# Modulation weights requested one step ahead in a two-layer hybrid decoder

## The chip, the cores and the metric

The kernel runs on one core of a Trainium2 chip. Its time is the device time of one execution in microseconds (us). Engines: PE is TensorE (matrix products), PEld its weight loads, DVE is VectorE, ACT is ScalarE, POOL is GpSimd. SP is the sync engine, whose queue issues most DMAs here. Less time is better.

## The reference

Two layers work on x of 1024 tokens by 1024 channels, in float32. Each layer computes

```
mod = silu(c) @ W_mod + b_mod             # W_mod is 1024 x 3072: shift, scale, gate
h = rms_norm(x, pre_gain) * (1 + scale) + shift
proj = h @ W_in                           # 1024 x 3088 columns, for three groups of heads
a = sliding-window attention, r = retention, g = gated linear attention, each times silu of a gate
x = x + gate * rms_norm(concat(a, r, g) @ W_out, post_gain)
```

The modulation is the same for all tokens: one row of 1024 numbers times a matrix of 12 MB per layer. Shift and scale of a layer are wanted before its first projection, the gate only after its output projection.

## The kernel before

Every product of the trunk is split into a high and a low part, so each weight block and each input are held twice, and a projection is three runs of eight products. Weights come in blocks of 256 columns. `load` (L467) brings a block in four pieces of 256 KB through a ring of five staging buffers (tag `st`, `stage`, `BST` = 5); ACT or DVE makes the high part, DVE or POOL the low part (L491, L481), and that frees the staging buffer. The converted block lies in a place of `arenas` until PE reads it.

The modulation that is not needed at the very start is computed beside the other stages by `mod_third(l, j)` (L344), for layer l and third j (0 shift, 1 scale, 2 gate). It works in two passes of 512 columns. A pass has eight steps k. A step brings a slice of `W_mod`, 128 rows by 512 columns, 256 KB, into a buffer of the same staging ring (SP queue, the kind `lwm`), and DVE multiplies it by one column of silu(c) and adds it to `acc` (L365 for the first step of shift and scale, L367 otherwise). After the eighth step PE sums `acc` over the partitions by products with ones (the closing products). `acc` exists once, so a pass begins its multiplies only when PE has read the pass before. Eight passes run this way: the gate of layer 0, scale and shift of layer 1 during layer 0, and the gate of layer 1 during layer 1.

The order of PE's instructions is written out by the program: generators ("jobs") emit their instructions when a planner's clock (`clk`) has advanced far enough. The clock grows by a cost for each product, `pump` looks for jobs that are due, and `accum` calls it after every 7 products of 256 columns or every 4 of 512. After each part of its work a job says with `yield lat(name, l)` how many planned us must pass before the next; the numbers stand in the table `L` (`@1` marks layer 1). In `mod_third`, `mod7` is the distance from the request of a slice to its multiply, `mod2` the distance from a multiply to the next request, and `mod3` that from the last multiply to the closing products. The flag `modh` of the shift lets the jobs that normalise and transpose tokens for layer 1 (`pre`, transposes at L176) go on; the flag `mod` of the gate lets the output projection begin.

Only PE is ordered by hand (`tc.manual_schedule(engines={PE})`). The instructions of SP, DVE, ACT and POOL are ordered by the framework when the program is built, by readiness and free buffers, with the written order as rank. Each engine then carries out its own list strictly in that order, and an issue on SP that waits for a staging buffer holds back what stands behind it.

Other names that the text uses: `attn_turn` is the softmax of the attention (DVE L934 copies scores, L936 takes the maximum, ACT L939 the exponentials). `aoS` is attention output kept in HBM, read back by SP and used by DVE at L1445. L1209 is the masking of retention scores on DVE.

Of the kernel before, what the change touches and what calls it, by code (L numbers as in the profile page):

```python
# [23 lines left out]
KT = D // P  # L24
# [65 lines left out]
def trunk(ctx: ExitStack, tc: tile.TileContext, ins, cst, out):  # L90
# [14 lines left out]
    def nm(s):  # L105
        uid[0] += 1
        return f"{s}_{uid[0]}"

    def t2(dt=F32):
        return gp.tile([P, 512], dt, tag="t2", name=nm("t2"), bufs=B2)  # L110
# [4 lines left out]
    def stage():  # L115
        return gp.tile([P, 512], F32, tag="st", name=nm("st"), bufs=BST)
# [7 lines left out]
    def aux(dt=F32):  # L124
        return ps.tile([P, 512], dt, tag="aux", name=nm("aux"), bufs=8 - MMB)
# [23 lines left out]
    def dma(k, dst, src):  # L149
        {"S": nc.sync, "A": A, "P": G}[EN[k]].dma_start(dst, src)  # L150
# [9 lines left out]
    def mult(dst, lhsT, rhs, start, stop, cost=None):  # L160
        T.matmul(dst, lhsT, rhs, start=start, stop=stop)  # L161
        if cost is not None:
            clk[0] += cost
            return
        n = 1
        for d in rhs.shape[1:]:
            n *= d
        c = n / 2400.0
        if rhs.dtype == F32R:
            c = max(c, 0.107 if lhsT.shape[-1] > 64 else 0.055)  # L170
        else:
            c = max(4 * c, 0.21 if n > 2 else 0.03)
        clk[0] += c
# [5 lines left out]
    def lat(key, l):  # L179

        return L[key + "@1"] if l and key + "@1" in L else L[key]

# [3 lines left out]
    def flag(name, lat=0.0):  # L186
        flags[name] = clk[0] + lat
# [75 lines left out]
    def mod_rows(l, j, eng=nc.sync):  # L263
        rows = gp.tile([16, P], F32, tag="row", name=nm("rows"), bufs=2)
        eng.dma_start(rows[0:8, :], b_mod[l:l + 1, j * D:(j + 1) * D].rearrange("o (k p) -> (o k) p", p=P))
        eng.dma_start(rows[8:16, :], pre_g[l:l + 1, :].rearrange("o (k p) -> (o k) p", p=P))
        return rows

    def mod_rows_t(rows, pool=aux):
        pr = pool()  # L270
        transp(pr[:, 0:16], rows, ident[0:16, 0:16])
        rc = small(16)
        V.tensor_copy(rc, pr[:, 0:16])
        return rc

    def mod_cols(l, j, hh, pm, rc):
        res = modc[(l, j)]
        ks = slice(4 * hh, 4 * hh + 4)
        if j == 0:
            V.tensor_tensor(res[:, ks], pm[:, 0:4], rc[:, ks], ALU.add)  # L280
        else:
            col = small(4)
            V.tensor_tensor(col, pm[:, 0:4], rc[:, ks], ALU.add)
            V.scalar_tensor_tensor(res[:, ks], col, 1.0, rc[:, 8 + 4 * hh:12 + 4 * hh], ALU.add, ALU.mult)

    def mod_tile(l, j):
        modc[(l, j)] = cp.tile([P, KT], F32, name=nm(f"mod{j}"), tag=f"mod{j}")
# [56 lines left out]
    def mod_third(l, j):  # L344
        wv = w_mod[l].rearrange("(p k) n -> p k n", k=KT)
        if j < 2:
            mod_tile(l, j)
            rows = mod_rows(l, j)
            yield lat("mod1", l)
            rc = mod_rows_t(rows)  # L350
        else:
            res = cp.tile([P, D], F32, name=nm("modg"), tag="modg")
            modg[l] = res
        for hh in range(2):
            c0 = j * D + 512 * hh
            acc = gp.tile([P, 512], F32, tag="acc", name=nm("acc"), bufs=1)
            if j == 2:
                G.memset(acc, 0.0)
                nc.sync.dma_start(acc[0:1, :], b_mod[l:l + 1, c0:c0 + 512])
            for k in range(KT):  # L360
                wt = stage()
                dma("lwm", wt, wv[:, k, c0:c0 + 512])
                yield lat("mod7", l)
                if k == 0 and j < 2:
                    V.tensor_scalar(acc, wt, c_act[:, k:k + 1], None, ALU.mult)  # L365
                else:
                    V.scalar_tensor_tensor(acc, wt, c_act[:, k:k + 1], acc, ALU.mult, ALU.add)  # L367
                yield lat("mod2", l)
            yield lat("mod3", l)
            pm = aux()  # L370
            if j < 2:
                for b in range(4):
                    mult(pm[:, b:b + 1], acc[:, b * P:(b + 1) * P], ones[:, 0:1], True, True)
                mod_cols(l, j, hh, pm, rc)
                if j == 0:
                    flag(("modh", l, hh), lat("mod4", l))
            else:
                mult(pm, ones, acc, True, True)
                gain = stage()
                nc.sync.dma_start(gain, post_g[l:l + 1, 512 * hh:512 * hh + 512].to_broadcast((P, 512)))  # L380
                V.tensor_tensor(res[:, 512 * hh:512 * hh + 512], pm, gain, ALU.mult)
            yield lat("mod5", l)
        flag(("mod", l, j), lat("mod6", l))

    def mod_all(l, js, after=None):
        if after is not None:
            yield (0.0, after)
        for j in js:
            yield from mod_third(l, j)
# [57 lines left out]
    def tables_T():  # L447

        for p in range(NP_):
            yield L["tt1"]  # L450
            rep_ = t2()
            V.tensor_copy(rep_.rearrange("p (s t h k) -> p s t h k", s=2, t=2, h=4),
                          sincos[:, 2 * p:2 * p + 2, :, 0:32].rearrange("p t s k -> p s t k").unsqueeze(3)
                          .to_broadcast((P, 2, 2, 4, 32)))
            yield L["tt2"]
            pt = aux()
# [127 lines left out]
    def pre(l, t, xt, early=False, soon=False):  # L584
# [9 lines left out]
        with ExitStack() as es:  # L594
# [3 lines left out]
            for j in range(2):  # L598
                if EN[f"xn{j}"] == "A" or early and XA[t][j] == "A" or soon and XA[t][j] == "A":
                    A.activation(xn[j], xt[j], AF.Copy, scale=r)  # L600
                else:
                    scaled[t] = V.tensor_scalar(xn[j], xt[j], r, None, ALU.mult)  # L602
        yield 0.5 if early else L["pf1"] if soon else lat("pre1", l)
        if early:
# [79 lines left out]
    def load_x(t, xt, eng_):  # L684
        for j in range(2):
            eng_.dma_start(xt[j], x_in[0, t * P:(t + 1) * P, 512 * j:512 * j + 512])

    def pre_first(t):
        xt = [t2(), t2()]
        load_x(t, xt, nc.sync)  # L690
        yield L["pf3"] + L["pf2"] * (t - 4)
        yield from pre(0, t, xt)
# [606 lines left out]
    def table_job():  # L1299
        more = True  # L1300
        yield (L["tb0"], ("hT", 0, TT))
        while more:
# [205 lines left out]
B2, B1, BS, BST, MMB, SMB = 12, 8, 11, 5, 3, 6  # L1508
EN = {"qst": "S", "smh": "S", "sml": "S", "sm0": "S", "sm1": "S", "lao": "S", "sao": "S", "lmix": "S", "ssg": "S", "lsg": "S", "ssr": "S", "lsr": "A", "lx": "S", "sx": "A", "lw": "S", "lwm": "S", "whi0": "V", "whi1": "A", "whi2": "A", "whi3": "A", "wlo0": "V", "wlo1": "G", "wlo2": "V", "wlo3": "G", "xn0": "V", "xn1": "V", "hlo0": "G", "hlo1": "V", "rot0": "V", "rot1": "V", "rdec": "V", "kslo": "V", "qslo": "V", "vlo": "G", "kT": "A", "qT": "A", "sprev": "A", "pn": "G", "pf0": "A", "aoc": "A", "hng": "V", "mh": "A", "gso": "V", "mg": "V", "mgl": "V", "rT": "A", "rv": "A", "gv": "A", "gk": "A", "ak0": "V", "ak1": "V", "ak2": "V", "ak3": "V", "kd0": "G", "kd1": "G", "kd2": "G", "kx1": "G", "kx2": "G", "kx3": "V", "kx4": "V", "qb": "G", "stx": "V"}
TURN = ("AV", "AV")  # L1510
L = {"tt1": 5.71, "tt2": 6.96, "tb1": 28.02, "tb2": 0.05, "pf3": 12.62, "pf1": 6.69, "pf2": 4.0, "mod1": 4.3, "mod2": 2.4, "mod3": 17.69, "mod4": 5.8, "mod5": 0.09, "mod6": 0.05, "pre1": 7.43, "kv1": 8.84, "kv2": 2.31, "aq1": 7.17, "aq7": 7.95, "ag1": 5.62, "aq2": 2.4, "aq6": 6.2, "aq3": 11.35, "aq4": 7.54, "aq5": 4.01, "hn1": 8.14, "hn2": 3.76, "gz1": 10.47, "gz2": 13.49, "gl1": 4.43, "gd3": 16.57, "gc1": 1.21, "gc2": 1.95, "gc3": 0.65, "gc4": 3.27, "gc6": 3.2, "gc5": 4.23, "rc1": 0.73, "rc2": 2.11, "rc3": 1.31, "rc4": 2.84, "fin1": 11.68, "lay1": 0.05, "mod2@1": 2.23, "mod3@1": 16.46, "mod5@1": 3.78, "mod6@1": 3.24, "pre1@1": 10.18, "kv1@1": 3.37, "kv2@1": 0.05, "aq1@1": 5.95, "aq7@1": 6.81, "ag1@1": 8.3, "aq2@1": 2.07, "aq6@1": 9.39, "aq3@1": 11.0, "aq4@1": 6.32, "aq5@1": 1.76, "hn1@1": 10.35, "hn2@1": 3.59, "gz1@1": 3.83, "gz2@1": 12.55, "gl1@1": 17.99, "gd3@1": 15.63, "gc1@1": 1.6, "gc2@1": 1.95, "gc3@1": 0.47, "gc4@1": 1.87, "gc6@1": 0.05, "gc5@1": 1.38, "rc1@1": 0.12, "rc2@1": 3.46, "rc3@1": 2.6, "rc4@1": 5.99, "fin1@1": 9.35, "lay1@1": 1.23, "gc7": 0.81, "gc7@1": 0.33, "tb0": 0.05, "mod7": 1.0, "mod7@1": 1.0}
CHUNK = 7
VDB = 8
VDF = 6
# [49 lines left out]
```

## Time and profile before

| | |
|---|---|
| median of 3 runs | 972.73 us (972.31 to 973.64) |
| profiled execution | 971.16 us, span 969.4 us, 1.8 us around it |
| PE busy | 951.3 us (98% of the span) |
| PEld busy | 829.4 us (86%) |
| DVE, ACT, POOL busy | 640.2, 410.1, 272.5 us |
| DMA | 140.30 MB, mean 145 GB/s |
| granted TensorE clock | 0.996 |

Times are counted from the start of the span. A row of a group gives line, engine, operation, written tile <- read tiles, shape and count, then busy us and mean ns of one, then the idle time of the engine just before these instructions and what ended it. A row of a wait list reads: who waited <- for whom: us in total, times, longest. A row of the timeline gives start, length, engine, line and operation, and in brackets the idle time before it. In the chain of waits a row gives start and length of the piece that the end depended on.

### The profile page before, as it was taken

Reading aid. Unit: us, or ns where it says so; the run is one execution under the profiler, and the core shown is the slowest. Engines: PE = TensorE matmul, PEld = TensorE weight load, DVE = VectorE, ACT = ScalarE, POOL = GpSimd, SP = SyncE. Lnnn points to the kernel's source line nnn. Section 1 sums busy time; section 2 is a strip of 40 time slices with the busy share of each in tenths; the row PEclk is TensorE's granted clock in tenths of the full one; section 3 lists DMA queues with packets and bytes.
Section 4 is the critical chain, followed back from the end, with each engine's and each line's share of the span. In section 5 each row is a group of like instructions: output and inputs, shape, how many; then the busy total and the mean of one; then the engine's idle time right before and its main releaser. Section 6 shows DMA issues by size and latency. Waiting matters only on the chain.

```text
span 969.4 us, 18061 instructions
## 1 busy us (share of the span) xinstructions
PE 951.3 (98%) x6513; PEld 829.4 (86%) x6513; DVE 640.2 (66%) x1525; ACT 410.1 (42%) x1119; POOL 272.5 (28%) x323
## 2 busy tenths in 40 slices
PE   6999999999999999999999999999999999999997
PEld 1799999989998877878889999998999887777886
DVE  6886857777777777655586485686776577763332
ACT  2777312354422666622455531134652166761111
POOL 3243011533430344511242110144423034441000
PEclk9999999999999999999999999999999999999999
DMA  9943314624335355677455160253222333555871
GB/s 313 320 146 110 111 56 129 187 77 112 115 102 150 98 168 180 218 242 237 172 166 172 50 180 22 83 155 92 80 86 77 120 88 105 158 174 174 261 238 65
DMA packets 124293, 140.30 MB, mean 145 GB/s; under 512 B 12734, under 2 KB 95528, under 8 KB 124204
## 3 DMA queue, kind: packets, MB, share of 16 engines
q1 hardware_dynamic: 116204, 127.43, 42.9%
q10 hardware_dynamic: 8000, 11.72, 3.4%
q8 instruction: 51, 0.84, 0.4%
q14 instruction: 38, 0.31, 0.1%
HBM read 102.42 MB, written 34.60 MB: 141 GB/s over the span
## 4 chain that ended last, share of the span: by engine, by line
PE 86%; DMA 7%; DVE 3%; issue 2%; POOL 1%; ACT 0%; SPq 0%; DVEq 0%; ACTq 0%; POOLq 0%
PE mm L161 67%; PE aux L161 15%; PE aux L176 4%; DMA wm<-in_w_mod_dram 2%; DMA t<-in_x_dram 1%; DMA st<-in_w_in_dram 1%; DMA xk<-in_x_dram 1%; DMA t<-aoS 1%; DMA st<-in_w_mod_dram 1%; POOL sm L529 1%; DVE acc L367 0%; DVE t L1292 0%; POOL arena L491 0%; DVE t L624 0%; DMA c_ident<-cst_ident_dram 0%
## 5 line engine op out<-in xcount | busy, mean ns | idle before, releaser
L161 PE MATMUL mm<-arena,arena 128*128 128x256 f32 (+2 forms) x1896 | 303.0, 315 | 1.4 <-ACT arena L628 0.7
L161 PE MATMUL mm<-arena 128*128 128x256 f32 (+2 forms) x1824 | 294.7, 317 | 0.0
L161 PEld LDWEIGHTS mm<-arena,arena 128*128 128x128 f32 x1896 | 261.8, 188 | 24.6 <-ACT arena L628 1.2
L161 PEld LDWEIGHTS mm<-arena 128*128 128x128 f32 x1824 | 255.4, 191 | 22.0 <-issue 1.2
L161 PE MATMUL mm<-arena,mx 128*128 128x512 f32 (+1 forms) x744 | 168.7, 386 | 0.0
L161 PEld LDWEIGHTS mm<-arena,mx 128*128 128x128 f32 x744 | 135.6, 188 | 29.1 <-issue 1.5
L529 POOL TENSOR_TENSOR sm<-sm,mhalf 128x4 f32<-128x4 f32 (+1 forms) x60 | 51.8, 863 | 294.8 <-DVE sm L528 285.3
L491 POOL TENSOR_TENSOR arena<-st,arena 128x512 fp32r<-128x512 f32 x55 | 80.3, 1467 | 91.3 <-ACT arena L145 34.7
L145 ACT ACTIVATE t<-aux 128x512 f32<-128x512 f32 (+1 forms) x96 | 48.7, 521 | 106.4 <-PE aux L176 44.9
L943 POOL TENSOR_TENSOR smx<-smx,sm 128x512 f32<-128x512 f32 x32 | 36.2, 1131 | 114.8 <-DVE sm L942 111.4
L491 DVE TENSOR_TENSOR arena<-st,arena 128x512 fp32r<-128x512 f32 x65 | 62.3, 969 | 4.7 <-PE mm L161 2.6
L145 ACT ACTIVATE arena<-st 128x512 fp32r<-128x512 f32 x82 | 48.5, 626 | 29.0 <-PE mm L161 13.0
L1247 ACT ACTIVATE t<-mm 128x512 f32<-128x512 f32 x30 | 17.9, 597 | 92.2 <-PE mm L161 40.3
L939 ACT ACTIVATE smx<-smx,sm 128x129 f32<-128x129 f32 x128 | 50.0, 393 | 14.0 <-DVE sm L936 13.9
L1248 DVE TENSOR_TENSOR t<-mm,modg 128x512 f32<-128x512 f32 x30 | 20.6, 689 | 48.6 <-ACT t L1247 48.5
L367 DVE SCALAR_TENSOR_TENSOR acc<-st,c_act,acc 128x512 f32<-128x512 f32 x60 | 47.3, 788 | 7.5 <-DMA st<-in_w_mod_dram 6.8
L1292 DVE SCALAR_TENSOR_TENSOR t<-t,sm,t 128x512 f32<-128x512 f32 x32 | 25.9, 846 | 39.7 <-DMA t<-xs 20.8
L176 PE MATMUL aux<-c_ident,t 128*128 128x128 f32 x288 | 45.5, 278 | 2.9 <-DVE t L602 2.9
L176 PEld LDWEIGHTS aux<-c_ident,t 128*128 128x128 f32 x288 | 34.9, 144 | 7.3 <-DVE t L602 4.2
L934 DVE COPY_PREDICATED smx<-c_curmask,aux 128x256 f32<-128x256 int32 x64 | 25.5, 447 | 15.0 <-ACT smx L145 10.4
L990 ACT ACTIVATE t<-aux 128x256 f32<-128x256 f32 x32 | 12.2, 382 | 54.1 <-PE aux L161 26.8
L995 DVE TENSOR_TENSOR t<-aux,sm 128x256 f32<-128x256 f32 x32 | 13.6, 425 | 30.8 <-POOL sm L529 30.8
(214 smaller groups left out, 1300.9 us busy)
## 6 DMA issues: line engine op xcount, KB each, us to landing
st<-in_w_in_dram SPq DMA_DIRECT2D x96, 256.0 KB
st<-in_w_mod_dram SPq DMA_DIRECT2D x64, 256.0 KB
mx<-mixS SPq DMA_DIRECT2D x30, 512.0 KB
mixS<-t SPq DMA_DIRECT2D x64, 128.0 KB
st<-in_w_out_dram SPq DMA_DIRECT2D x32, 256.0 KB
mixS<-t SPq DMA_DIRECT2D x32, 256.0 KB
wm<-in_w_mod_dram SPq DMA_DIRECT2D x12, 512.0 KB
t<-in_x_dram SPq DMA_DIRECT2D x24, 256.0 KB
```

Source lines behind the costliest of these rows:

```text
L145: A.activation(dst, src, AF.Copy)
L161: T.matmul(dst, lhsT, rhs, start=start, stop=stop)
L176: T.transpose(dst, src, idn)
L367: V.scalar_tensor_tensor(acc, wt, c_act[:, k:k + 1], acc, ALU.mult, ALU.add)
L491: i = (G if first == 0 and kc in LOG else V if first == 0 else eng(f"wlo{kc}")).tensor_tensor(wt[:, 1, 2 * kc:2 * kc + 2, 0:256], st, f(hi ...
L529: after[2] = G.tensor_tensor(r, r, mhalf[:, :w], ALU.pow)
L934: V.copy_predicated(sv, curmask.unsqueeze(1).to_broadcast((P, 2, P)), pv[:, :, n // P - 1, :])
L939: A.activation(sm[:, h, :], sm[:, h, :], AF.Exp, bias=mx[:, h:h + 1], accum_out=sums[:, h:h + 1])
L943: eng("pn").tensor_tensor(sm[:, :, 0:128], sm[:, :, 0:128], rs.unsqueeze(2).to_broadcast((P, 4, P)), ALU.mult)
L1247: A.activation(yg, pm, AF.Square, accum_out=ss[:, nh:nh + 1])
L1248: V.tensor_tensor(yg, pm, modg[l][:, 512 * nh:512 * nh + 512], ALU.mult)
L1292: V.scalar_tensor_tensor(xt[j], yg[j], r, xt[j], ALU.mult, ALU.add)
```

## The change

In the loop over k, the load of slice k+1 is written ahead of the planned wait and of the multiply of slice k; the first slice is requested ahead of the loop. Two staging buffers are then named by a pass at a time where there was one. In the planner's table, `mod7` goes from 1.0 to 0.05 in both layers, and `mod2` from 2.4 (layer 0) and 2.23 (layer 1) to 2.9. Nothing else differs.

```diff
             if j == 2:
                 G.memset(acc, 0.0)
                 nc.sync.dma_start(acc[0:1, :], b_mod[l:l + 1, c0:c0 + 512])
+            def fetch(k):
+                w_ = stage()
+                dma("lwm", w_, wv[:, k, c0:c0 + 512])
+                return w_
+
+            coming = fetch(0)
             for k in range(KT):
-                wt = stage()
-                dma("lwm", wt, wv[:, k, c0:c0 + 512])
+                wt, coming = coming, fetch(k + 1) if k + 1 < KT else None
                 yield lat("mod7", l)
...
-L = {... "mod2": 2.4, ... "mod2@1": 2.23, ... "mod7": 1.0, "mod7@1": 1.0}
+L = {... "mod2": 2.9, ... "mod2@1": 2.9, ... "mod7": 0.05, "mod7@1": 0.05}
```

More of the change, by code (lines that the diff above doesn't have):

```diff
@@ L1510 @@
 TURN = ("AV", "AV")
-L = {"tt1": 5.71, "tt2": 6.96, "tb1": 28.02, "tb2": 0.05, "pf3": 12.62, "pf1": 6.69, "pf2": 4.0, "mod1": 4.3, "mod2": 2.4, "mod3": 17.69, "mod4": 5.8, "mod5": 0.09, "mod6": 0.05, "pre1": 7.43, "kv1": 8.84, "kv2": 2.31, "aq1": 7.17, "aq7": 7.95, "ag1": 5.62, "aq2": 2.4, "aq6": 6.2, "aq3": 11.35, "aq4": 7.54, "aq5": 4.01, "hn1": 8.14, "hn2": 3.76, "gz1": 10.47, "gz2": 13.49, "gl1": 4.43, "gd3": 16.57, "gc1": 1.21, "gc2": 1.95, "gc3": 0.65, "gc4": 3.27, "gc6": 3.2, "gc5": 4.23, "rc1": 0.73, "rc2": 2.11, "rc3": 1.31, "rc4": 2.84, "fin1": 11.68, "lay1": 0.05, "mod2@1": 2.23, "mod3@1": 16.46, "mod5@1": 3.78, "mod6@1": 3.24, "pre1@1": 10.18, "kv1@1": 3.37, "kv2@1": 0.05, "aq1@1": 5.95, "aq7@1": 6.81, "ag1@1": 8.3, "aq2@1": 2.07, "aq6@1": 9.39, "aq3@1": 11.0, "aq4@1": 6.32, "aq5@1": 1.76, "hn1@1": 10.35, "hn2@1": 3.59, "gz1@1": 3.83, "gz2@1": 12.55, "gl1@1": 17.99, "gd3@1": 15.63, "gc1@1": 1.6, "gc2@1": 1.95, "gc3@1": 0.47, "gc4@1": 1.87, "gc6@1": 0.05, "gc5@1": 1.38, "rc1@1": 0.12, "rc2@1": 3.46, "rc3@1": 2.6, "rc4@1": 5.99, "fin1@1": 9.35, "lay1@1": 1.23, "gc7": 0.81, "gc7@1": 0.33, "tb0": 0.05, "mod7": 1.0, "mod7@1": 1.0}
+L = {"tt1": 5.71, "tt2": 6.96, "tb1": 28.02, "tb2": 0.05, "pf3": 12.62, "pf1": 6.69, "pf2": 4.0, "mod1": 4.3, "mod2": 2.9, "mod3": 17.69, "mod4": 5.8, "mod5": 0.09, "mod6": 0.05, "pre1": 7.43, "kv1": 8.84, "kv2": 2.31, "aq1": 7.17, "aq7": 7.95, "ag1": 5.62, "aq2": 2.4, "aq6": 6.2, "aq3": 11.35, "aq4": 7.54, "aq5": 4.01, "hn1": 8.14, "hn2": 3.76, "gz1": 10.47, "gz2": 13.49, "gl1": 4.43, "gd3": 16.57, "gc1": 1.21, "gc2": 1.95, "gc3": 0.65, "gc4": 3.27, "gc6": 3.2, "gc5": 4.23, "rc1": 0.73, "rc2": 2.11, "rc3": 1.31, "rc4": 2.84, "fin1": 11.68, "lay1": 0.05, "mod2@1": 2.9, "mod3@1": 16.46, "mod5@1": 3.78, "mod6@1": 3.24, "pre1@1": 10.18, "kv1@1": 3.37, "kv2@1": 0.05, "aq1@1": 5.95, "aq7@1": 6.81, "ag1@1": 8.3, "aq2@1": 2.07, "aq6@1": 9.39, "aq3@1": 11.0, "aq4@1": 6.32, "aq5@1": 1.76, "hn1@1": 10.35, "hn2@1": 3.59, "gz1@1": 3.83, "gz2@1": 12.55, "gl1@1": 17.99, "gd3@1": 15.63, "gc1@1": 1.6, "gc2@1": 1.95, "gc3@1": 0.47, "gc4@1": 1.87, "gc6@1": 0.05, "gc5@1": 1.38, "rc1@1": 0.12, "rc2@1": 3.46, "rc3@1": 2.6, "rc4@1": 5.99, "fin1@1": 9.35, "lay1@1": 1.23, "gc7": 0.81, "gc7@1": 0.33, "tb0": 0.05, "mod7": 0.05, "mod7@1": 0.05}
 CHUNK = 7
```

## The prediction

> **What bounds the kernel now.** I read the head of the page first, then the busy time of the engines by stage, then the list of who waited for whom, and at last the instructions around the longest wait that the change could touch.
>
> ```profile
> span 969.4 us, 18061 instructions
> PE 951.3 (98%) x6513; PEld 829.4 (86%) x6513; DVE 640.2 (66%) x1525; ACT 410.1 (42%) x1119; POOL 272.5 (28%) x323
> ...
> L367 DVE SCALAR_TENSOR_TENSOR acc<-st,c_act,acc 128x512 f32<-128x512 f32 x60 | 47.3, 788 | 7.5 <-DMA st<-in_w_mod_dram 6.8
> ```
>
> PE is busy for 951.3 of 969.4 us. The last row is the step that the change feeds: 60 of the 64 multiplies by a slice of modulation weights (the other four are the first of a pass). Before them DVE stands idle for 6.8 us until a slice lands. That is the whole of what an earlier request can take off DVE. Whether it can come off the end is a question of PE, so next comes the table by stage (each line: stretch, its length, then busy us of PE, PEld, DVE, ACT, POOL).
>
> ```profile
> 22.50:88.00 65.50, 64.57 (x458) 55.66 (x457) 51.47 (x118) 48.70 (x126) 20.58 (x19) 0.97 0.60 196
> 88.00:148.00 60.00, 60.00 (x518) 58.52 (x517) 42.44 (x129) 18.59 (x36) 6.50 (x5) 1.00 0.33 99
> 148.00:188.00 40.00, 39.62 (x325) 37.80 (x323) 31.61 (x84) 11.42 (x25) 12.07 (x10) 1.00 0.51 152
> 188.00:332.00 144.00, 143.59 (x1029) 128.90 (x1025) 105.43 (x266) 62.68 (x172) 48.89 (x68) 1.00 0.39 114
> 332.00:430.00 98.00, 97.50 (x614) 75.69 (x614) 70.15 (x133) 54.30 (x170) 40.61 (x45) 1.00 0.63 192
> 430.00:558.00 128.00, 127.54 (x784) 113.43 (x783) 75.25 (x162) 58.72 (x159) 32.14 (x32) 1.00 0.50 165
> 558.00:960.00 402.00, 402.00 (x2737) 351.88 (x2736) 246.01 (x598) 148.98 (x416) 103.39 (x123) 1.00 0.41 127
> ```
>
> The modulation steps that change lie between 88 and 676 us. There PE is idle for 0 + 0.38 + 0.41 + 0.50 + 0.46 = 1.75 us, after 558 us not at all, and between 22.5 and 88 us it is idle for 0.93. So all waiting of PE from 22.5 to 960 us is 2.68 us, 0.28% of the span: the most that any change of order can give back. The waits of PE from 88 us on have these names:
>
> ```profile
> PE aux L176 <- DVE smx L934: 0.5, 1, 0.5
> PE mm L161 <- DVE t L1009: 0.5, 1, 0.5
> PE aux L161 <- DVE t L1209: 0.4, 1, 0.4
> PE aux L161 <- ACT t L145: 0.2, 1, 0.2
> PE aux L161 <- DVE sc L1140: 0.2, 1, 0.2
> ```
>
> Only the third leads back to a modulation slice. The chain of waits and the SP queue show it.
>
> ```profile
> 157.21 0.76 DVE acc L367
> 157.99 5.75 DMA st<-in_w_mod_dram
> ...
> 166.56 1.94 PE aux L161 x14
> ```
> ```profile
> 150.02 0.33 SPq L150 DMA_DIRECT2D st<-in_w_mod_dram  x1
> 152.95 0.38 SPq L150 DMA_DIRECT2D st<-in_w_in_dram  x1
> ...
> 155.08 0.38 SPq L150 DMA_DIRECT2D st<-in_w_in_dram  x1
> ...
> 156.41 1.17 SPq L150 DMA_DIRECT2D st<-in_w_in_dram  x2
> 157.99 0.34 SPq L150 DMA_DIRECT2D st<-in_w_mod_dram  x1
> ```
> ```profile
> 163.83 0.75 DVE L367 SCALAR_TENSOR_TENSOR acc<-st,c_act,acc 128x512 f32<-128x512 f32 x1 [4.18 <-DMA st<-in_w_mod_dram]
> ```
>
> Slice 4 of the second pass goes out at 150.02, then four weight blocks, then slice 5 at 157.99. Multiply 4 ends at 157.21 + 0.76 = 157.97, and 0.02 us later SP issues slice 5: it waited for a place in the ring of five staging buffers that the multiply of slice 4 gave back. Its data are used 5.8 us after issue, and DVE idles 4.18 us. PE loses 0.38 of that.
>
> **The change part by part.** It adds no instruction: 64 loads of 256 KB and 64 multiplies remain. *The request.* The load of slice k+1 is now written ahead of multiply k. Only PE follows the written order; on the other queues the framework orders by readiness, with the written order as rank. So a load already goes out early when a buffer is free: the bias row of the second pass is written ahead of its slices, but goes out at 149.25, while slices 0 to 3 went out at 107.90:
>
> ```profile
> 107.90 2.90 SPq L150 DMA_DIRECT2D st<-in_w_mod_dram  x4
> ...
> 149.25 0.25 SPq L359 DMA_DIRECT2D acc<-in_b_mod_dram  x1
> ```
>
> What really changes is the rank of one slice against a weight block written within the step in between. At 150 us slice 5 would come ahead of the four blocks and take a buffer at 152.95, one multiply ahead of each block. With the 5.8 us of this case it lands at 158.7, 0.8 us after multiply 4 instead of 5.9 us, so most of the 4.18 goes, and with it PE's wait: -0.38 us, between -0.38 and 0. The other three DVE waits (6.8 - 4.2 = 2.6 us) are ahead of no PE wait in the list: 0.
>
> *What is late next.* Each of those blocks now takes the buffer of the next multiply: the first goes out at 155.08 instead of 152.95, 2.1 us later, the second 1.3, and the last at 157.97 after multiply 4, 0.8 later. SP's waits price it:
>
> ```profile
> SPq L150 <- DVE acc L367: 17.7, 27, 3.4
> ```
>
> 27 waits of 0.66 us in the mean, at most 3.4. Behind the waiting issue stand the other issues of SP (reads and stores of intermediate tensors), and ACT, POOL and DVE, which convert the blocks. The cover is how long the converted weights lie before PE reads them. These blocks' last conversion is the DVE row at 170.22, ending 170.90; PE's first product of 512 columns with them starts at 183.11.
>
> ```profile
> 170.22 0.68 DVE L491 TENSOR_TENSOR arena<-st,arena 128x512 fp32r<-128x512 f32 x1
> 183.11 1.18 PE L161 MATMUL mm<-arena,arena 128*128 128x512 f32 x4
> ```
>
> That is 12.2 us against 3.4 us: I take 0. Without that cover it would be up to 3.4 us.
>
> *The planner's distances.* The planned gap from load to multiply falls from 1.0 to 0.05, the gap after the multiply rises from 2.4 (layer 0) or 2.23 (layer 1) to 2.9. A step can only run where the planner looks, every 7 products of 0.107 us, 0.749 us. Rounded up, a step of layer 0 falls from 1.498 + 2.996 to 0.749 + 2.996 us; one of layer 1 stays at 1.498 + 2.247 = 3.745. So two passes in layer 0 shrink by up to 8 x 0.749 = 6.0 planned us each, and the later passes keep their length but start up to 12 us earlier. That moves eight groups of closing products in PE's order, no more:
>
> ```profile
> L161 PE MATMUL aux<-c_ones,acc x32: 166/250/271, 273.1 to 473.1; 128*128 128x1 f32 x32
> L161 PE MATMUL aux<-acc,c_ones x8: 590/592/595, 147.6 to 675.3; 128*128 128x512 f32 x8
> ```
>
> They cost the same at another place. PE's four other waits in the list above (0.5, 0.5, 0.2, 0.2) may vanish or grow as the order around them shifts. The trace cannot show the new order; the nearest rows are these waits themselves: -1.4 if all go, +1.4 if all double. I take 0, since nothing in the chain ties them to a slice. What precedes the transposes of layer 1 is wanted earlier too, but PE is full there.
>
> **The sum**: 971.16 us is this execution (969.4 of span and 1.8 around it); -0.38 gives 970.78. The median of the runs is 972.73, 1.57 higher; on it the forecast is 972.35, rounded 972.3.
>
> **The rivals.** *Faster: the busy PE row hides waiting.* Weight loading is busy for 37.80 of the 40 us from 148 to 188, so 2.20 us are free there. If they are all waiting that ends with the DVE stall, the time is 972.73 - 2.20 = 970.5. For it: this is the stage with the 4.18 us. Against it: the stage from 88 to 148 has no idle PE at all and still 60 - 58.52 = 1.48 us free in 60. [...]
>
> *No effect.* Slices stay behind blocks because buffers, not rank, decide: 972.7. For it: slices 0 to 3 above went out 42 us ahead without the change.
>
> *Slower: a slice gets ahead of a read that PE depends on.* In the attention stage SP issues five output-weight blocks, then the read of the attention result, and DVE waits for it:
>
> ```profile
> 349.64 4.39 SPq L150 DMA_DIRECT2D st<-in_w_out_dram  x5
> 354.13 1.77 SPq L150 DMA_DIRECT2D t<-aoS  x2
> ```
> ```profile
> 360.11 0.69 DVE L1445 SCALAR_TENSOR_TENSOR t<-t,t 128x512 f32<-128x512 f32 x1 [4.62 <-DMA t<-aoS]
> ```
>
> DVE's softmax work (L934) queues behind, and PE's 0.5 us wait for L934, first in the list above, shows that no cover is left. One more slice ahead is 256 KB at the stage's 192 GB/s, 1.4 us, straight onto the end; with two, or one and its buffer wait of up to 3.4 us, 972.73 + 2.8 = 975.5, up to 977.5. It decides as soon as a slice stands between 349.6 and 354.1 us. For it: slice 6 of that pass follows the blocks now and would be first to rise. Against it: the pass also starts earlier, and may be over by then.
>
> **How the numbers follow.** Forecast 0.50 (its own range 971.0 to 974.4), no effect 0.14, faster 0.11, slower 0.25. A measurement of this kernel can tell about 0.2%, 1.95 us, from no change: below 970.8 is faster, above 974.7 slower. The forecast and no effect lie within, the rivals outside: 0.11, 0.64, 0.25. The range takes the faster rival's 970.5 in and most of the slower's: 970.3 to 977.2.
>
> **What would show it.** Right: the 6.8 us of DVE waiting for slices falls under 2; slice 5 goes out ahead of the four blocks near 150 us; PE's wait for L1209 is gone; the second closing products come before 207 us and the last before 472; PE's waits stay under 3 us after 22.5. Wrong: a new wait of PE of over 1 us for softmax or converted weights, ACT or DVE waits for weight blocks that grow, or a span that moves while PE's waits don't.

## The result, and the profile after

The changed kernel takes 973.92 us (median of 19 runs), the kernel before 971.6 us (19 runs beside them). The ratio is 1.0025, 95% interval 1.0018 to 1.0033: slower by 2.4 us, 1.7 to 3.2. The profiled execution took 973.54 us, with a span of 971.8.

The head of the page after, and the multiply by a slice, which is now line 372 (lines from 367 on have moved down by 5):

```profile
span 971.8 us, 18069 instructions
PE 949.4 (98%) x6513; PEld 828.4 (85%) x6513; DVE 640.7 (66%) x1525; ACT 409.8 (42%) x1119; POOL 271.6 (28%) x323
...
L372 DVE SCALAR_TENSOR_TENSOR acc<-st,c_act,acc 128x512 f32<-128x512 f32 x60 | 47.6, 793 | 8.5 <-DMA st<-in_w_mod_dram 7.8
```

DVE waits for slices for 7.8 us where it was 6.8: the request did not take that waiting away. (Over all profiled executions it is 6.8 to 7.8 us before and 7.2 to 10.8 us after.) The stages after, with the columns of the prediction's table:

```profile
88.00:148.00 60.00, 60.00 (x516) 58.21 (x515) 42.22 (x128) 19.11 (x37) 8.03 (x6) 1.00 0.34 102
148.00:188.00 40.00, 39.69 (x326) 38.14 (x326) 32.60 (x87) 12.04 (x26) 11.84 (x10) 1.00 0.52 152
188.00:332.00 144.00, 142.93 (x1031) 128.57 (x1030) 107.13 (x267) 62.07 (x171) 49.64 (x68) 1.00 0.39 113
332.00:430.00 98.00, 96.55 (x609) 75.22 (x609) 70.66 (x134) 53.39 (x169) 39.69 (x45) 1.00 0.60 185
430.00:558.00 128.00, 127.74 (x779) 112.81 (x774) 73.54 (x161) 59.05 (x159) 29.31 (x31) 1.00 0.53 169
558.00:960.00 402.00, 401.92 (x2737) 351.76 (x2736) 245.73 (x597) 148.74 (x415) 105.59 (x124) 1.00 0.42 128
```

PE now waits 0 + 0.31 + 1.07 + 1.45 + 0.26 + 0.08 = 3.17 us after 88 us, against 1.75. The increase lies in two stages. The list of PE's waits names them:

```profile
PE aux L176 <- DVE smx L939: 1.2, 1, 1.2
PE aux L176 <- DVE t L1000: 1.1, 1, 1.1
...
PE aux L161 <- DVE t L1214: 0.3, 1, 0.3
PE aux L161 <- ACT t L145: 0.3, 1, 0.3
PE mm L161 <- DMA mx<-mixS: 0.3, 1, 0.3
```

The two of over 1 us are the instructions below, of PE and of DVE:

```profile
272.89 0.44 PE L176 MATMUL aux<-c_ident,t 128*128 128x128 f32 x2 [1.07 <-DVE t L1000]
...
353.45 1.07 PE L176 MATMUL aux<-c_ident,smx 128*128 128x128 f32 x8 [1.18 <-DVE smx L939]
```
```profile
272.41 0.42 DVE L1000 TENSOR_TENSOR t<-aux,sm 128x256 f32<-128x256 f32 x1 [1.12 <-POOL sm L534]
...
349.56 3.39 DVE L372 SCALAR_TENSOR_TENSOR acc<-st,c_act,acc 128x512 f32<-128x512 f32 x4
352.86 0.78 DVE L939 COPY_PREDICATED smx<-c_curmask,aux 128x256 f32<-128x256 int32 x2
```

These transposes are written into accumulator banks, the five tiles `aux` of the program, and the program writes a bank anew only when another engine has read it. At 273 us L1000 reads such a bank and gives it back; it ends at 272.41 + 0.42 = 272.83 us, and PE, which has waited 1.07 us, starts at 272.89. L1000 runs 1.12 us after its predecessor on DVE, because POOL works in between. At 353 us the softmax work L939 stands on DVE behind four modulation multiplies in a row. Neither waits for a slice.

The request itself, on the SP queue in the second pass:

```profile
151.59 3.25 SPq L150 DMA_DIRECT2D st<-in_w_mod_dram  x2
...
156.64 0.38 SPq L150 DMA_DIRECT2D st<-in_w_in_dram  x1
...
157.97 1.94 SPq L150 DMA_DIRECT2D st<-in_w_in_dram  x3
160.33 0.34 SPq L150 DMA_DIRECT2D st<-in_w_mod_dram  x1
```
```profile
165.33 0.75 DVE L372 SCALAR_TENSOR_TENSOR acc<-st,c_act,acc 128x512 f32<-128x512 f32 x1 [4.12 <-DMA st<-in_w_mod_dram]
```

Slice 5 now goes out ahead of the four blocks, as forecast. But slice 6 goes out behind them, at 160.33, and DVE waits 4.12 us for it. The stall of 4.18 us moved on by one slice.

### The profile page after: what moved, and what is told of

It reads as the page before. It is cut to its first block, busy times and chain, and to the rows that moved or that the text cites. A ratio compares the mean times of both kernels' runs of the same rounds, so it can differ in the third digit from the quotient of the medians.

```text
span 971.8 us, 18069 instructions
## 1 busy us (share of the span) xinstructions
PE 949.4 (98%) x6513; PEld 828.4 (85%) x6513; DVE 640.7 (66%) x1525; ACT 409.8 (42%) x1119; POOL 271.6 (28%) x323
## 4 chain that ended last, share of the span: by engine, by line
PE 83%; DMA 7%; DVE 4%; ACT 2%; issue 2%; POOL 1%; SPq 0%; DVEq 0%; POOLq 0%; ACTq 0%
PE mm L161 65%; PE aux L161 13%; PE aux L176 4%; DMA wm<-in_w_mod_dram 2%; ACT smx L944 1%; DMA xk<-in_x_dram 1%; DVE acc L372 1%; DMA mx<-mixS 1%; DMA st<-in_w_in_dram 1%; DMA t<-t 1%; POOL sm L534 1%; DMA st<-in_w_mod_dram 1%; DMA sm<-in_attn_sinks_dram 0%; DVE arena L496 0%; DMA mixS<-t 0%
## 5 line engine op out<-in xcount | busy, mean ns | idle before, releaser
L496 DVE TENSOR_TENSOR arena<-st,arena 128x512 fp32r<-128x512 f32 x65 | 59.8, 932 | 4.8 <-PE mm L161 2.9
L939 DVE COPY_PREDICATED smx<-c_curmask,aux 128x256 f32<-128x256 int32 x64 | 25.6, 447 | 16.8 <-ACT smx L145 11.1
L1000 DVE TENSOR_TENSOR t<-aux,sm 128x256 f32<-128x256 f32 x32 | 13.6, 425 | 32.0 <-POOL sm L534 30.9
```

The source lines that it names most:

```text
L496: i = (G if first == 0 and kc in LOG else V if first == 0 else eng(f"wlo{kc}")).tensor_tensor(wt[:, 1, 2 * kc:2 * kc + 2, 0:256], st, f(hi ...
L939: V.copy_predicated(sv, curmask.unsqueeze(1).to_broadcast((P, 2, P)), pv[:, :, n // P - 1, :])
```

## The experiments

Two theories stood at the start. *Q*: the request order does the harm, since a slice stands ahead of a read or a block that PE needs. *P*: the planner's distances do it, by moving PE's and DVE's instructions.

A table of all timed kernels first. "Waiting" is the PE idle time between 88 and 960 us in the kernel's profile (872 less the busy time of that stretch). "Clock" counts the places in that stretch where the granted clock fell to one half. The intervals are 95%, each against runs of the kernel before on the same chip. Waiting and clock are those of one execution each. Passes are counted in order of time: 1 and 2 are the gate of layer 0, 3 and 4 the scale, 5 and 6 the shift, 7 and 8 the gate of layer 1. Layer 0's entries in the table serve passes 1 and 2, layer 1's the other six.

| kernel | time / before | waiting, us | clock |
|---|---|---|---|
| before (profile shown) | 1 | 1.75 | 0 |
| changed (profile shown) | 1.0025 (1.0018 to 1.0033) | 3.17 | 0 |
| c_after, the changed kernel again | 1.0018 (1.0006 to 1.0030) | 3.15 | 0 |
| e_code, fetch alone | 0.9998 (0.9983 to 1.0013) | 0.78 | 0 |
| e_table, distances alone | 1.0042 (1.0027 to 1.0056) | 4.77 | 0 |
| e_l0, fetch, distances of layer 0 | 1.0004 (0.9994 to 1.0015) | 1.96 | 1 |
| e_l1, fetch, distances of layer 1 | 0.9985 (0.9977 to 0.9994) | 0.94 | 0 |
| e_close3, one group of products moved | 1.0038 (1.0025 to 1.0051) | 3.89 | 1 |
| e_pass34, old distances in passes 3, 4 | 1.0009 (1.0001 to 1.0018) | 1.32 | 0 |
| e_both, these two | 1.0021 (1.0011 to 1.0032) | 1.97 | 1 |
| e_trans4, one pair of transposes moved | 1.0019 (1.0008 to 1.0030) | 3.42 | 0 |
| e_mend, e_trans4 and e_pass34 | 1.0001 (0.9992 to 1.0010) | 1.09 | 0 |
| e_ring6, six staging buffers | 1.0100 (1.0085 to 1.0116) | 8.68 | 2 |
| e_own, slices in buffers of their own | 1.0122 (1.0101 to 1.0142) | 7.79 | 3 |

**The two parts of the change, each alone.** e_code has the new loop and the old distances:

```diff
-"mod2": 2.9, "mod2@1": 2.9, "mod7": 0.05, "mod7@1": 0.05
+"mod2": 2.4, "mod2@1": 2.23, "mod7": 1.0, "mod7@1": 1.0
```

> The fetch written one step ahead, with the planner's distances of before. PE's, ACT's and POOL's orders of instructions are then almost those of before (PE's wholly), and only SP issues slices earlier. Theory Q (the request order does the harm: a slice stands ahead of the read or the block that PE needs, and a stall moves on): 1.2 to 2.3 us slower than before, ratio 1.0012 to 1.0024, with waits of PE of about 1 us near 273 and 353 us. Theory P (the planner's distances do it, by moving PE's and DVE's instructions): within 0.5 us of before, ratio 0.9995 to 1.0005, PE's waits after 88 us about 1.75 us in all as before; DVE's wait for a slice near 160 us moves one slice on but ends no wait of PE over 0.5 us.

e_table has the old loop, which requests a slice in the step that uses it, and the new distances:

```diff
-            coming = fetch(0)
             for k in range(KT):
-                wt, coming = coming, fetch(k + 1) if k + 1 < KT else None
+                wt = stage()
+                dma("lwm", wt, wv[:, k, c0:c0 + 512])
                 yield lat("mod7", l)
```

> The loop of before, each slice requested in the step that uses it, with the changed kernel's planner distances (load to multiply 0.05, after the multiply 2.9). PE then has exactly the changed kernel's order. Theory P: 1.5 to 2.5 us slower than before, ratio 1.0015 to 1.0026, with the waits of PE for DVE of about 1.1 us near 273 us (t, layer 0's gating) and 1.2 us near 353 us (smx). Theory Q: within 0.5 us of before and neither wait over 0.6 us. If both parts are needed: half, about 1.0012, as one of the two waits shows.

Set beside the trace of the kernel before row by row, e_code leaves PE's order exactly as it was and moves 18 of SP's 546 issues and 11 of DVE's 1525 instructions. e_table has exactly the changed kernel's order on PE: 89 of PE's 6513 rows stand elsewhere, in 28 places, and 75 instructions of DVE. The one is level with before (between 1.7 us faster and 1.3 us slower), the other 4.1 us slower (2.6 to 5.4). PE's busy time between 88 and 960 us, in e_code and then in e_table:

```profile
88.00:960.00 872.00, 871.22 (x6006) 767.48 (x6005) 573.78 (x1371) 355.18 (x979) 245.07 (x283) 1.00 0.44 137
```
```profile
88.00:960.00 872.00, 867.23 (x5978) 763.63 (x5978) 570.73 (x1368) 354.51 (x977) 243.64 (x282) 1.00 0.45 137
```

So theory P holds: the distances do the harm, by moving PE's and DVE's instructions. Both kernels missed in size: e_code waits 0.78 us where 1.75 was expected, and e_table lost more than the 1.5 to 2.5 us expected for it. With the new distances the earlier request gives back some 2 us of what they cost (1.0042 against 1.0018 on the same chip); alone it gives nothing that can be measured. Why it helps only there was not tested.

**The distances, layer by layer.** e_l0 puts layer 1's two entries back, e_l1 layer 0's.

> The changed kernel with the new planner distances for layer 0's passes only; layer 1's are those of before. Under theory P the time lies between: layer 0's entries move PE's instructions from 206 us on, so the wait of 1.1 us near 273 us stays and the one of 1.2 us near 353 us goes: about 1.0 to 1.3 us slower than before, ratio 1.0010 to 1.0013. Under theory Q the same time as the changed kernel, ratio about 1.0024, since the request order is the changed kernel's.

> The changed kernel with the new planner distances in layer 1's passes only; layer 0's are those of before. It is the other half of the kernel with layer 0's entries alone. Theory P: the wait near 353 us (1.2) is there, the one near 273 us is not (under 0.4); PE's waiting after 88 us 2.0 to 2.4 us, the time 1.0005 to 1.0013 of before. If both waits are there, or neither, the split of the loss between the two entries is wrong.

e_l0 has the wait of 1.07 us near 273 us and not the one near 353 us, as expected; its time came out lower than expected (1.0004, with an interval that holds both). e_l1 has neither wait where it was to have the second, and is the one kernel here that beats before: by 0.15%; a loss of 0.05 to 0.13% had been expected. So the wait near 353 us was not layer 1's, as I had it. It shows only where both layers' entries are new. Losses of the two halves don't add up: 0.4 and -1.4 us apart, 2.4 together.

**Which wait, by moving one thing.** In e_close3 the third pass's closing products are written ahead of the transposes that wait at 273 us, in e_pass34 passes 3 and 4 get their old distances (which puts the fourth pass's closing products back behind the transposes of smx), e_both does both.

```diff
+            early = 0.9 if (l, j, hh) == (1, 1, 0) else 0.0
+            due = clk[0] + lat("mod3", l)
-            yield lat("mod3", l)
+            yield lat("mod3", l) - early
...
-                yield lat("mod7", l)
+                yield 1.0 if (l, j) == (1, 1) else lat("mod7", l)
...
-                yield lat("mod2", l)
+                yield 2.23 if (l, j) == (1, 1) else lat("mod2", l)
```

> The changed kernel with the closing products of the third pass alone (near 273 us) written 0.9 planned us earlier: in PE's order they then stand directly ahead of the two transposes of the gated t, where before they stood behind them; the rest of PE's order, SP's and ACT's are the changed kernel's. Theory P (the wait near 273 us is cover that the closing products gave and that the planner's new order took away): PE's wait for t there falls from 1.07 to about 0.1 us, the wait of 1.2 us near 353 us stays, PE's waiting after 88 us falls from about 3.15 to 2.2 us and the time to about 1.0012 of before (0.9 us less than the changed kernel). Rival (DVE is late by itself and what PE does ahead of it doesn't matter, or the closing products are then waited for themselves): the wait stays over 0.6 us under one name or another, and the time is the changed kernel's, 1.0018 to 1.0025.

> The changed kernel with the distances of before (1.0 and 2.23) in the third and fourth pass alone. In PE's order one thing moves: the fourth pass's closing products (near 337 us) go back behind the transposes of smx that stood behind them. Theory P: the waits near 337 (0.27) and 353 us (1.18) fall under 0.3 in sum, the one near 273 us (1.07) stays, waiting after 88 us falls from about 3.15 to 1.8 us, and the time to 1.0008 of before (1.3 us less than the changed kernel). Rival (the wait near 353 us comes from the four multiplies in a row that stand ahead of the softmax work in DVE's order, wherever the closing products stand): it stays at 0.8 us or more, and the time within 0.4 us of the changed kernel's.

> Both of these edits: third pass's closing products ahead of the transposes of t, fourth pass's behind those of smx. Theory P: both waits gone, PE's waiting after 88 us 0.7 to 1.0 us as in the kernel with the fetch alone, and the time of before or 0.5 us under it, ratio 0.9990 to 1.0005. If it is 1.0015 or more, the two waits are not what the changed kernel lost.

e_close3 was a miss. Its line 1005 is the changed kernel's line 1000:

```profile
274.38 1.38 PE L161 MATMUL aux<-c_ones,acc 128*128 128x1 f32 x8 [1.07 <-DVE t L1005]
```

The same wait of 1.07 us now stands in front of the closing products. They need an accumulator bank too, and L1000 is what gives one back. So it is a bank that PE waits for at this place, and not the tile that it transposes. And the time went up instead of down, for which this profile has a second reason, the granted clock (the seventh number, PEclk):

```profile
272.00:274.00 2.00, 1.31 (x16) 1.03 (x16) 0.69 (x3) 0.89 (x3) 1.01 (x1) 1.00 0.25 74
...
275.00:278.00 3.00, 3.00 (x15) 3.00 (x16) 2.90 (x12) 0.66 (x2) 1.08 (x3) 0.50 0.00 0
278.00:278.50 0.50, 0.50 (x4) 0.50 (x4) 0.50 (x3) 0.28 (x1) 0.50 (x2) 0.64 0.60 209
278.50:279.00 0.50, 0.50 (x7) 0.50 (x6) 0.13 (x1) 0.00 (x0) 0.39 (x2) 1.00 0.17 53
```

Behind the wait the clock is at one half for about 3.4 us; from 275 to 278 us, at 0.50, PE runs 15 products, and 27 from 279 to 282 us, at 1.00. Half the speed for 3.4 us is worth an estimated 1.7 us. e_pass34 did what theory P said of it: the waits near 337 and 353 us are gone when the fourth pass's closing products (8 rows of PE) stand behind the transposes again, waiting fell to 1.32 us, and the time lies 0.9 to 1.6 us under the changed kernel (1.0009 against its 1.0018 and 1.0025; 1.3 us was expected). The rows of PE, now without a wait in front:

```profile
336.37 1.32 PE L176 MATMUL aux<-c_ident,smx 128*128 128x128 f32 x8
337.53 0.95 PE L161 MATMUL aux<-c_ones,acc 128*128 128x1 f32 x8
...
351.77 1.06 PE L176 MATMUL aux<-c_ident,smx 128*128 128x128 f32 x8
```

All 20 profiles agree on this place: the wait near 353 us is there (1.18 to 1.99 us) in the nine in which these closing products stand ahead of the transposes of smx near 337 us, and in none of the other eleven.

e_both missed its 0.9990 to 1.0005: with the wait at 273 us still there, now behind a different name, and in the profiled execution the clock falling behind it, it is at 1.0021.

Since a bank is what is missing at 273 us, e_trans4 puts products that need none ahead: the waiting pair of transposes goes behind the next 7 products and the closing products. e_mend adds the edit of e_pass34.

```diff
-        yield lat("hn1", l)
+        yield lat("hn1", l) + (1.8 if (l, t, kt0) == (0, 4, 6) else 0.0)
```

> The changed kernel with one pair of transposes (the normed output of the fifth tile, those that wait near 273 us) written 1.8 planned us later, behind the next 7 products and the third pass's closing products. SP's and ACT's orders are the changed kernel's. Theory P, as it stands after the closing products were moved (PE needs an accumulator bank there that DVE's L1000 gives back 1.07 us late; whatever stands first waits): PE now has 0.8 us of products ahead of the next need of a bank, the wait falls from 1.07 to 0.2 to 0.4 us, the granted clock does not fall near 275 us, and the time is 0.8 to 1.3 us less than the changed kernel: 1.0008 to 1.0015 of before. Rival (DVE itself runs later with PE, as the same chain of waits is merely met later): 0.8 us or more of waiting at that place, time as the changed kernel's.

> The same edit, and the distances of before in the third and fourth pass (the kernel with those alone had 1.07 us of wait left at 272 us, and none near 337 and 353). Theory P: PE's waiting after 88 us 0.5 to 0.9 us, against 1.75 of before and 3.15 of the changed kernel; no fall of the granted clock after 88 us; time 0.9990 to 1.0003 of before, about the kernel with the fetch alone. If it is 1.0010 or more, something is left that PE's waits don't show.

In e_trans4 the wait at 273 us is gone, and nothing is won:

```profile
271.37 1.10 PE L161 MATMUL mm<-arena 128*128 128x256 f32 x7
272.51 1.05 PE L161 MATMUL aux<-c_ones,acc 128*128 128x1 f32 x8
...
336.93 1.05 PE L161 MATMUL aux<-c_ones,acc 128*128 128x1 f32 x8 [0.80 <-ACT t L145]
```

At 336.93 a wait that was 0.27 us is now 0.80, and the one near 353 us stays at 1.18. The rival is right in the time and in its reason, though not in the place: the lag is met later. With passes 3 and 4 put back as well (e_mend) it is met nowhere: 1.09 us of waiting (0.5 to 0.9 was expected), and the time of before, as expected.

**More room for the slices.** e_ring6 has six staging buffers for five, with the changed kernel's order on PE. e_own has the fetch with the old distances, and two buffers for slices beside the ring of five.

```diff
-B2, B1, BS, BST, MMB, SMB = 12, 8, 11, 5, 3, 6
+B2, B1, BS, BST, MMB, SMB = 12, 8, 11, 6, 3, 6
...
-                w_ = stage()
+                w_ = gp.tile([P, 512], F32, tag="sw", name=nm("sw"), bufs=2)
```

> The changed kernel with six staging buffers where there are five; PE's order is the changed kernel's. Theory Q (slices and weight blocks wait for one ring, and that is what ends at PE): DVE's waits for slices fall from 7.8 to under 3 us, the table read near 329 us goes out earlier, and PE's waits at 168 (0.31) and 353 us (1.18) go: 1.3 us less than the changed kernel, about 1.0008 of before. Theory P: DVE's waits for slices fall as well, but the wait near 273 us stays at 1.07, and the one near 353 us at 0.8 or more: within 0.5 us of the changed kernel.

> The fetch with the planner's distances of before, and the slices in two staging buffers of their own beside the ring of five, so that no slice waits for a block's buffer. PE's order is that of before. Theory A (slices come late because they share the ring): DVE's waits for slices fall from 7.9 to under 3 us, PE's waiting after 88 us stays under 0.8, time 0.9985 to 1.0003 of before. Theory B (an earlier request makes the multiply stand earlier in DVE's order, ahead of its landing, as with the ring of six): DVE's waits for slices grow to 9 us or more, new waits of PE over 1 us show behind them, time 1.003 or more.

Both became much slower than the kernel before, by 9.7 and 11.9 us; the sixth buffer costs some 7.5 us against the changed kernel. Neither expectation for e_ring6 covers that; for e_own it is its theory B. DVE waits longer for slices, 15.4 us in e_ring6 and 17.6 in e_own:

```profile
L372 DVE SCALAR_TENSOR_TENSOR acc<-sw,c_act,acc 128x512 f32<-128x512 f32 x60 | 52.1, 869 | 17.9 <-DMA sw<-in_w_mod_dram 17.6
```

In e_ring6 a multiply of the first pass stands ahead of the last two of the gate work L1014, all of which it followed in the changed kernel, and waits; PE waits for L1014 (first the row of DVE, then that of PE):

```profile
91.72 0.75 DVE L372 SCALAR_TENSOR_TENSOR acc<-st,c_act,acc 128x512 f32<-128x512 f32 x1 [3.20 <-DMA st<-in_w_mod_dram]
```
```profile
96.92 1.31 PE L161 MATMUL mm<-arena,arena 128*128 128x256 f32 x9 [1.66 <-DVE t L1014]
```

**The same kernels again.** The changed kernel was run beside the others, and then, for their profiles, three more executions of it, one of e_l1 and two of the kernel before.

> The changed kernel once more, beside the others on one chip: ratio 1.0018 to 1.0033 as measured. Its profile tells which waits of PE come back: theory P and Q both expect the two of about 1.1 us near 273 and 353 us again. If they are gone and the time is the same, neither of them is the cause. The first 88 us should not differ from before in the mean, since no engine's order differs there: the 1.5 us by which the first profile of after was later at 70 us should not come back each time.

> The changed kernel once more, for its profile alone. Waits of PE explain 1.4 us of the 2.4 us that it lost. If the rest is the clock, the granted clock falls to 0.50 for about 3.4 us behind the wait near 273 us in some of the executions (3 of the 7 kernels profiled so far with that wait show it), and such an execution has 1.7 us more between 182 and 320 us; if no execution of it shows this, the rest stays unexplained.

> A second execution of the changed kernel. Either the clock falls behind the wait near 273 us, with 1.7 us more in that stage, or the waits are again 3.1 to 3.2 us after 88 us and nothing else differs.

> A third execution of the changed kernel, with the same two outcomes: a fall of the clock to 0.50 near 275 us and 1.7 us more, or waits of 3.1 to 3.2 us after 88 us and no fall.

> The kernel with the new distances in layer 1's passes only, which came out 0.15 per cent under before, for its profile alone on this chip: if waits and clock are the whole of it, PE's waiting after 88 us is again under 1.2 us, no wait is over 0.7 us, and the clock does not fall after 88 us.

> The kernel before, for its profile. In the one profile shown of it PE reaches 139 us earlier than nearly all variants, by 1.1 us in the mean, though the orders of all engines are the same up to 150 us. If that was one lucky execution, this one is 0.5 to 2 us later there; if it is as early again, the changed kernel loses something in the first 139 us too. After 88 us: waits of PE 1.5 to 2.0 us in all, none over 0.6, no fall of the clock.

> A second execution of the kernel before, with the same two outcomes: 0.5 to 2 us later at 139 us than the profile shown (chance of that execution), or as early as it (a loss of the changed kernel that its order doesn't show). Waits after 88 us 1.5 to 2.0 us, the clock does not fall there.

Waiting after 88 us was 3.17, 3.15, 4.85, 2.83 and 2.95 us in five executions of the changed kernel, 1.75, 2.55 and 2.09 in three of the kernel before: 3.39 and 2.13 in the mean, 1.3 us apart. The two waits near 273 and 353 us are in all five (0.80 to 1.07, and 1.18 or 1.19) and in none of the three. The clock fell once in the five, and not near 273 us as I had expected, but behind the wait at 168 us, after an execution's slice came later than usual (a DVE stall of 5.28 us):

```profile
168.78 0.77 PE L161 MATMUL aux<-t,t 128*128 128x64 f32 x4 [1.47 <-DVE t L1214]
...
171.00:175.00 4.00, 4.00 (x25) 4.00 (x25) 3.39 (x9) 0.00 (x0) 2.66 (x2) 0.66 0.65 181
```

p_l1 was a miss: its one execution (974.14 us) has a wait of 0.99 us at 337 us that the profiled execution of e_l1 did not have, and the clock falls behind it. None of the 11 runs of e_l1 took more than 971.62 us, so its 0.9985 tells nothing of such an execution; how often one comes is open. For the two executions of before I had expected no wait over 0.6 us; they have 1.23 and 1.07 us at 168 us.

The same product of PE, where all orders up to it are equal, starts at 139.2, 139.5 and 141.5 us in the kernel before and at 140.8, 140.2, 140.3, 141.3 and 141.3 in the changed one. The means are 0.7 us apart, but each kernel spreads over more than that, so whether part of the 2.4 us arises there stays open. From that product to the end it is 830.2, 830.8 and 830.2 us against 831.0, 831.2, 834.5, 830.8 and 831.0: 1.3 us in the mean, 0.8 in the median. The 834.5 is the execution in which the clock fell, and it fell behind the wait at 168 us, which the kernel before has too; without it the means are 0.6 us apart, and the means of the waiting 0.9. So the profiles show 0.6 to 1.3 us of the 2.4; where the rest arises stays open.

## Why the prediction was wrong

The forecast was 0.38 us less than before, 972.3 us; the kernel is 2.4 us slower. The forecast started from the median of three runs, 972.73 us; 19 runs give 971.6, and from there it would have been 971.2. That 973.92 lies inside the range given is in part the luck of that start: the sign was wrong. Step by step:

- **What can be won.** That all waiting of PE (2.68 us) bounds a gain held: the best variant won 1.4 us. It bounds no loss, and the text used it as if the small waits also made the risk small.
- **The request.** Slice 5 did rise ahead of the blocks. The step "so most of the 4.18 goes" failed: I asked what would be late next among the blocks, not among the slices. Slice 6 took slice 5's place behind them, and DVE's waits are 7.8 us instead of under 2. PE's wait at 168 us did not go: 0.31 to 1.47 us in the changed kernel, 0.38 to 1.23 in the kernel before. A forecast gain of 0.38 us, read from one execution, was inside what that wait varies by from one execution to the next. In two more executions of the kernel before it is 1.07 and, on this row, 1.23:

```profile
167.70 0.77 PE L161 MATMUL aux<-t,t 128*128 128x64 f32 x4 [1.23 <-DVE t L1209]
```

- **The later blocks.** Cost 0 was right: in no profile of the changed kernel does PE wait for a converted weight after 88 us, and e_code, which has this edit, costs nothing that can be measured.
- **The planner's distances.** This is the step that failed. The premise, that passes of layer 0 shrink by up to 6 planned us, was wrong: from the first to the last multiply of the first pass the planner's own clock runs 27.30 before and 27.41 after. The planner does not step on a grid of 0.749; transposes and other small products advance its clock too, so in the first pass the gap from load to multiply was mostly 1.07, not 1.498, and a whole step stayed at 3.9. Closing products came at most 2.6 planned us earlier, not 12. And "that moves eight groups of closing products in PE's order, no more" was wrong as well: such small shifts moved 89 of PE's rows, products of the trunk and transposes among them, and in the whole change 82 of DVE's instructions. I took 0, with a bound of +1.4 made of waits that existed before. What came were waits that had not existed: 1.07 us for an accumulator bank and 1.18 us for softmax. In place of 0, the distances alone cost 4.1 us (e_table), and 2.4 with the earlier request. The mean of the waits rose by 1.3 us (0.9 without the execution in which the clock fell), just inside the bound; the rest of the 2.4 us is not shown. The bound did not know of the clock either, which fell in one of five executions.
- **The rivals.** The slower rival had the right sign, and its place came true: slice 6 of that pass goes out at 353.18 us, ahead of the output-weight blocks. But in the profile shown it cost nothing there. DVE's wait for the attention result is 1.77 us after, against 4.62 before, and PE's old wait of 0.47 us for softmax at 364 us is gone (two rows of SP, one of DVE):

```profile
353.18 0.42 SPq L150 DMA_DIRECT2D st<-in_w_mod_dram  x1
353.69 3.41 SPq L150 DMA_DIRECT2D st<-in_w_out_dram  x4
```
```profile
362.01 0.69 DVE L1450 SCALAR_TENSOR_TENSOR t<-t,t 128x512 f32<-128x512 f32 x1 [1.77 <-DMA t<-aoS]
```

  In one of the five executions (p_after1) this place did cost PE something: DVE waits 2.80 us for that slice and 1.66 us for the attention result behind it, and PE then 0.84 us for softmax (two rows of DVE, one of PE). How much of this the order makes, and how much a slow transfer, was not separated.

```profile
362.20 0.75 DVE L372 SCALAR_TENSOR_TENSOR acc<-st,c_act,acc 128x512 f32<-128x512 f32 x1 [2.80 <-DMA st<-in_w_mod_dram]
...
365.80 0.69 DVE L1450 SCALAR_TENSOR_TENSOR t<-t,t 128x512 f32<-128x512 f32 x1 [1.66 <-DMA t<-aoS]
```
```profile
369.63 0.63 PE L176 MATMUL aux<-c_ident,smx 128*128 128x128 f32 x4 [0.84 <-DVE smx L939]
```

  The wait that ended at 353.45 us came before that slice could matter. In e_code the same four multiplies stand ahead of the softmax work and PE does not wait (two rows of DVE, one of PE):

```profile
346.47 3.26 DVE L372 SCALAR_TENSOR_TENSOR acc<-st,c_act,acc 128x512 f32<-128x512 f32 x4
349.65 0.78 DVE L939 COPY_PREDICATED smx<-c_curmask,aux 128x256 f32<-128x256 int32 x2
```
```profile
350.24 1.06 PE L176 MATMUL aux<-c_ident,smx 128*128 128x128 f32 x8
```

  After the change DVE starts these 3.1 us later (349.56 for 346.47), PE reaches its transposes only 2.0 us later (353.45 less 1.18, for 350.24): the difference, and 0.13 us by which the four take longer, make the wait. The rival of a faster kernel by hidden waiting has no support: where e_code has no wait at 168 us at all it is not faster than before.
- **What would show it wrong** was named rightly: a new wait of PE of over 1 us for softmax is there. Of the signs of being right only one came, slice 5 ahead of the blocks.

## What to carry to other kernels

When a change alters numbers from which an order is planned, compare the orders first and price them: here the part that looked like a detail, four numbers in a table, made the loss, and the load that was meant, alone, did nothing measurable. Where PE is full, the waits that a new order makes are not bounded by the waits that the old one has (4.77 us in e_table, against 1.75); and a wait taken away at one place counts only if the engine behind it is not late at the next (in e_trans4 the wait of 1.07 us at 273 us went, the one near 337 us rose from 0.27 to 0.80, and the time stayed at 1.0019 of before). One profile of each kernel does not price a wait that hangs on a transfer: three of the same kernel gave 0.38, 1.07 and 1.23 us.

## What the runs showed of the hardware

Between 88 and 960 us the granted clock fell to one half, for about 3.4 us (once, in e_own, for 6.8), only behind waits of PE of 0.99 us or more. It did so behind all five waits of 1.7 us or more (1.73 to 2.53, in e_ring6 and e_own) and behind 5 of 25 between 0.9 and 1.7 us. Half the clock for 3.4 us is worth an estimated 1.7 us, if PE runs at half its speed there. The sizes fit: e_own waits 7.0 us longer than e_code and has 13.7 us at half clock, worth 6.8, together 13.8, and its profiled execution took 14.1 us longer. So a wait of PE of about 1 us can cost an estimated 2.7. Why one does and another doesn't was not tested.

More staging buffers made the kernel slower: one more by some 7.5 us against the changed kernel, two of their own for the slices by some 12 us against e_code. With one buffer more, the multiply at 91.72 us has an earlier place in DVE's order and waits 3.20 us for its data there; L1014 is queued behind, and PE waits 1.66 us for it. In all, the waits for slices are 15.4 us with one buffer more, against 7.2 to 10.8 us in five executions of the changed kernel.
